# Openings of modulated stages: weight splits pulled forward, none among the normed tiles, gated products spread

## The chip, the cores and the metric

One core of one Trainium2 chip runs the whole program. The metric is device time in microseconds of one execution; the time before is a median of three runs, and one more execution was recorded by the hardware profiler.

## The reference, cut to what matters

The program is two transformer blocks of depth 2 on 256 tokens of width 1024, in fp32. Three of the six sublayer kinds open with the same step, and the change touches only that step:

```
mod = (silu(c) @ ada_w[layer] + ada_b[layer])           # shift, scale, gate for 3 sublayers
h = rms_norm(x, norm_g[layer, i]) * (1 + scale_i) + shift_i
x = x + 0.5 * gate * ((silu(h @ Wa) * (h @ Wb)) @ w_down)   # feed-forward, d_ff = 2816
x = x + gate * diff_attention(h, ...)                       # layer 0
x = x + gate * hgrn2(h, ...)                                # layer 1
```

The six sublayers with a modulation run first, in the order ffn00, attn1, ffn01, ffn10, hgrn, ffn11. The second block (attn2, peer0, conv, peer1) has no modulation, and the change doesn't touch it.

## The kernel before

**Tiling.** Activations lie feature-major: 8 tiles of 128 features x 256 tokens, `xt`. Every product is done in three passes of fp32r: activations and weights are each split into a high part (`xh`, `whi`) and a low part (`xl`, `wlo`), and `mm3` issues high-high, low-high, high-low. A weight *piece* is 128 x 1024 (8 blocks of 128 x 128). Its split is one ACT copy (`whi`) and, after that, one DVE subtraction (`wlo`). A *product* of one piece is 8 x 3 = 24 matmuls. Pieces and products are numbered from 0 in each stage, so that piece 7 is the eighth.

**The order of splits.** All engines execute in the order in which the program writes their instructions. `take` fetches the next piece; before it returns, it writes splits of the coming pieces, as many as `self.ahead` allows beyond the piece taken and as the buffers have room for: six buffers in a feed-forward stage (3 base, 3 of the stage), five in attn1, four in hgrn. The plan of pieces also has *ada* rows in it, from the ninth piece of a stage on: one DVE multiply-and-sum of 128 x 1024 each, for the modulation of a later stage. They are executed in their turn among the splits.

**The opening**, `enter`. The norm's scale (one number per token) isn't known when a stage begins, since it needs the last tile of `xt`. So the first four products are done on tiles that are not normed (`unnormed`: gain only, two extra columns for the shift), and corrected by `complete` after the end. In order: `group` does products 0 and 1 together, k by k; `rstd` (four small matmuls on the sum of squares `ss`, then Ln and Exp on ACT and three small DVE steps, `rsq`); product 2; `rstd_rows` (four matmuls that spread the scale over the partitions, an ACT copy); product 3; `normed_pair`, which makes the 8 normed tiles (DVE `t`, ACT `xh`, DVE `xl` for each) while products 4 and 5 run on them k by k, as they come. In ffn00, the first stage, the squares were summed by PE, and `rstd` has no matmuls of its own.

**After the opening** come the four `complete` (DVE product and a column copy, ACT addition), and in a feed-forward stage `glu(f)`: ACT `sa` (silu, which needs a load of ACT's tables), DVE `t` = sa x pb, ACT `gh`, DVE `gl`. Products 6 and on use four PSUM banks in turn: product 10 writes the bank of product 6, 12 that of 8.

**How far ahead.** `AHEAD = (2, 3, 3, 3)` is the value of `ahead` for the group, product 2, product 3 and the normed pair; afterwards it is 100 (as many as there is room for). Counting `take`'s condition through, the splits stand thus in a feed-forward stage: to piece 3 in front of the group, 4 and 5 in front of product 2, 6 in front of product 3, and 7 and 8 in `normed_pair`, between the first `t` and the first `xh`; 9 to 11 in front of product 6, after `glu` 0, 1 and 2.

Of the kernel before, what the change touches and what calls it, by code (L numbers as in the profile page):

```python
# [83 lines left out]
LAST = 2  # L84
PEER_LAST = 3

AHEAD = (2, 3, 3, 3)


N_FREE, N_SHARED = 11, 48  # L90
# [246 lines left out]
def moving(pool, n, name):  # L337

    t = pool.tile([P, MOVE + n * T], F32R, name=name)
    return t[:, MOVE:].rearrange("p (a b) -> p a b", b=T)  # L340


class Kernel:
# [515 lines left out]
    def enter(self, names, dest):  # L859

        self.ahead = AHEAD[0]
        ps = self.group(names[:2], self.cols, "e")
        y = self.rstd()
        self.ahead = AHEAD[1]
        ps.append(self.features(*names[2], self.cols, "e"))
        self.rstd_rows(y)
        self.ahead = AHEAD[2]
        ps.append(self.features(*names[3], self.cols, "e"))
        self.ahead = AHEAD[3]
        two = self.normed_pair(names[4:6])  # L870
        self.ahead = 100
        return [self.complete(p, d) for p, d in zip(ps, dest)] + two
# [80 lines left out]
    def ffn(self, s):  # L953
        nc, wk = self.nc, self.wk
        layer, sub = SUB[s]
        self.banks(p=range(4), x=range(4, 8), e=range(4), n=[4, 5], ms=[6, 7])
        with self.tc.tile_pool(name=s, bufs=1) as pool:
            gh = moving(pool, KF, "gh")
            gl = moving(pool, KF, "gl")

            def glu(f, pa, pb):
                sa = pool.tile([P, T], F32, name="sa", bufs=2)
                nc.scalar.activation(sa, pa[:, :T], AF.Silu)
                g = wk.tile([P, T], F32, name="t", bufs=3)
                nc.vector.tensor_mul(g, sa, pb[:, :T])
                self.halves(gh[:, f], gl[:, f], g)

            un = [pool.tile([P, T], F32, name="un", bufs=4) for _ in range(4)]
            first = self.enter([(s + "_in", i) for i in range(6)], un)
            for f in range(3):  # L970
                glu(f, first[2 * f], first[2 * f + 1])
            for f in range(3, KF):
                pa = self.features(s + "_in", 2 * f)
                pb = self.features(s + "_in", 2 * f + 1)
                glu(f, pa, pb)
            nc.scalar.preload_act_table_set(LN_EXP)
            gt = self.gate(layer, sub, 0.5)
            if self.next is not None:
                self.lead(self.next)
            py = {}  # L980
            for i, (j, k) in enumerate(DOWN):
                if i % 8 == 0:
                    h, l = self.take(s + "_dn", i // 8)
                if k == 0:
                    py[j] = self.bank("x")
                self.mm3(py[j][:, :T], h[:, i % 8], l[:, i % 8], gh[:, k], gl[:, k], k == 0, k == KF - 1)
                if k == KF - 1:
                    self.resid(j, py[j][:, :T], gt)
# [1070 lines left out]
```

## Time and profile before

| | |
|---|---|
| median of 3 runs | 2886.76 us (2880.81 to 2913.92) |
| the profiled execution, its own time | 2896.64 us |
| its span in the profile | 2894.9 us |
| PE busy | 2833.7 us, 98% of the span |
| DVE, ACT busy | 2175.1 us (75%), 1667.1 us (58%) |

The span runs from the first to the last instruction. PE is TensorE's matmuls, PEld its weight loads, DVE is VectorE, ACT ScalarE. The share of busy time is a mean over all stages; the openings are short stretches of some 25 us each.

### The profile page before, as it was taken

What the parts mean: (1) busy time and instruction counts of PE and PEld (TensorE: products, weight loads), DVE (VectorE), ACT (ScalarE), POOL (GpSimd) and SP (SyncE); (2) the same over time, 40 slices, a digit from 0 to 9 for tenths busy, and PEclk for the clock granted to TensorE, in tenths of its full rate; (3) what the DMA queues carried; (4) which work ended last, traced back from release to release, by engine and by line L of the source; (5) the groups of instructions that cost most, each with busy time, mean ns of one, the idle gap of its engine ahead of it and who ended that gap; (6) DMA issues with size and microseconds to landing.
All of it is one profiled execution on the core that took longest, in us unless ns stands there. A gap on an engine that the chain in (4) does not pass through costs nothing.

```text
span 2894.9 us, 61164 instructions
## 1 busy us (share of the span) xinstructions
PE 2833.7 (98%) x24416; PEld 2787.4 (96%) x24416; DVE 2175.1 (75%) x4491; ACT 1667.1 (58%) x3234; POOL 12.2 (0%) x20
## 2 busy tenths in 40 slices
PE   5999999999999999999999999999999999999999
PEld 5999899999999999799999999999999999999999
DVE  6877788788797656779889755656879889865654
ACT  4456655454566544664688655545464688755553
POOL 0000000000000000000000000000000000000000
PEclk9999999999999999999999999999999999999999
DMA  7985469779543654155544555666445544555664
GB/s 270 332 326 181 145 236 334 281 259 337 193 145 135 201 183 158 53 176 190 185 163 162 173 192 196 213 196 217 156 168 190 190 161 161 170 195 193 214 196 148
DMA packets 158991, 577.17 MB, mean 199 GB/s; under 512 B 17649, under 2 KB 19825, under 8 KB 158321
## 3 DMA queue, kind: packets, MB, share of 16 engines
q1 hardware_dynamic: 156096, 565.25, 58.0%
q0 software_dynamic: 1280, 6.30, 0.6%
q8 instruction: 191, 3.13, 0.4%
q10 hardware_dynamic: 1328, 1.71, 0.2%
q14 instruction: 96, 0.78, 0.1%
HBM read 570.57 MB, written 2.62 MB: 198 GB/s over the span
## 4 chain that ended last, share of the span: by engine, by line
PE 93%; DVE 3%; ACT 2%; issue 1%; DMA 1%; ACTq 0%; DVEq 0%
PE bank L247 93%; DVE wlo L247 1%; DVE xl L247 1%; DMA params<-par 1%; ACT whi L247 1%; DVE t L247 1%; DVE ada_scr L247 1%; ACT un L247 0%; ACT xh L247 0%; ACT L247 0%; DMA raw<-ffn_in 0%; ACT gh L247 0%; ACT hx L247 0%; DVE ss L247 0%; DVE xt L247 0%
## 5 line engine op out<-in xcount | busy, mean ns | idle before, releaser
L247 PE MATMUL bank<-xh,whi 128*128 128x256 f32 (+1 forms) x6272 | 1769.9, 282 | 12.5 <-ACT xh L247 8.7
L247 PE MATMUL bank<-xl,whi 128*128 128x256 f32 (+1 forms) x6272 | 1748.8, 279 | 11.6 <-DVE xl L247 10.9
L247 PE MATMUL bank<-xh,wlo 128*128 128x256 f32 (+1 forms) x6272 | 1746.1, 278 | 2.2 <-DVE wlo L247 2.2
L247 DVE TENSOR_TENSOR wlo<-raw,whi 128x1024 fp32r<-128x1024 f32 x932 | 1134.2, 1225 | 511.2 <-ACT whi L247 503.9
L247 ACT ACTIVATE whi<-raw 128x1024 fp32r<-128x1024 f32 x932 | 972.8, 1056 | 676.4 <-PE bank L247 575.6
L247 PEld LDWEIGHTS bank<-xh,whi 128*128 128x128 f32 x6272 | 1186.4, 189 | 19.1 <-ACT xh L247 10.2
L247 PEld LDWEIGHTS bank<-xl,whi 128*128 128x128 f32 x6272 | 1186.7, 189 | 15.7 <-DVE xl L247 14.3
L247 PEld LDWEIGHTS bank<-xh,wlo 128*128 128x128 f32 x6272 | 1187.3, 189 | 2.8 <-DVE wlo L247 2.8
L247 PE MATMUL bank<-gh,whi 128*128 128x256 f32 x704 | 196.9, 280 | 0.0
L247 PE MATMUL bank<-gl,whi 128*128 128x256 f32 x704 | 196.9, 280 | 0.0
L247 PE MATMUL bank<-gh,wlo 128*128 128x256 f32 x704 | 196.9, 280 | 0.0
L247 DVE SCALAR_TENSOR_TENSOR ada_scr<-raw,cact 128x1024 f32<-128x1024 f32 x144 | 175.6, 1219 | 8.3 <-ACT cact L247 6.1
L247 ACT ACTIVATE ql<-q,gl 128x128 f16<-128x128 f16 x512 | 162.5, 395 | 0.0
L247 ACT ACTIVATE gh<-t 128x256 fp32r<-128x256 f32 x88 | 36.8, 418 | 195.2 <-DVE t L247 195.2
L247 PEld LDWEIGHTS bank<-gh,wlo 128*128 128x128 f32 x704 | 133.7, 190 | 0.0
L247 PEld LDWEIGHTS bank<-gh,whi 128*128 128x128 f32 x704 | 132.9, 189 | 0.0
L247 PEld LDWEIGHTS bank<-gl,whi 128*128 128x128 f32 x704 | 132.1, 188 | 0.0
L247 ACT ACTIVATE slots<-bank 128x256 f32<-128x256 f32 (+38 forms) x296 | 86.4, 294 | 16.2 <-PE bank L247 15.8
L247 PE MATMUL bank<-oh,whi 128*128 128x256 f32 x256 | 73.4, 287 | 0.2 <-ACT hx L247 0.2
L247 PE MATMUL bank<-qh,pm 128*128 128x128 f16 x512 | 72.9, 222 | 0.3
L247 PE MATMUL bank<-ql,pm 128*128 128x128 f16 x512 | 71.5, 219 | 0.1
L247 PE MATMUL bank<-ol,whi 128*128 128x256 f32 x256 | 71.4, 279 | 0.0
(235 smaller groups left out, 2546.8 us busy)
## 6 DMA issues: line engine op xcount, KB each, us to landing
raw<-peer_u SPq DMA_DIRECT2D x256, 512.0 KB, 3.3
raw<-peer_v SPq DMA_DIRECT2D x256, 512.0 KB, 3.7
raw<-ffn_in SPq DMA_DIRECT2D x176, 512.0 KB, 5.1
raw<-ada SPq DMA_DIRECT2D x144, 512.0 KB, 5.3
raw<-ffn_dn SPq DMA_DIRECT2D x88, 512.0 KB, 5.3
raw<-peer_q SPq DMA_DIRECT2D x32, 512.0 KB, 3.4
raw<-conv_in SPq DMA_DIRECT2D x24, 512.0 KB, 4.4
raw<-attn_qk SPq DMA_DIRECT2D x16, 512.0 KB, 4.3
```

The lines of the kernel that those rows point to most:

```text
L247: result = real(*args, **kw)
```

## The change

It does four things. In the stages with a modulation, `ahead` is 4 during the group, so that pieces 4 and 5 are split in front of products 0 and 1 (where the buffers have room). `rstd` is written in the middle of the group, ahead of its fifth k, except in ffn01 and ffn11. `ahead` is 0 in the normed pair, so that no piece is split there: 7 and 8 come after it, in the next `take`, which is product 6's. And `glu(1)` and `glu(2)` no longer stand in front of product 6: `glu(1)` is written after product 6, `glu(2)` after product 8.

```diff
-AHEAD = (2, 3, 3, 3)
+AHEAD = (4, 3, 3, 0)
+
+STAT = 4
...
     def enter(self, names, dest):
 
         self.ahead = AHEAD[0]
-        ps = self.group(names[:2], self.cols, "e")
-        y = self.rstd()
+        found = []
+
+        def statistics(k):
+            if k == STAT and self.stage not in ("ffn01", "ffn11"):
+                found.append(self.rstd())
+
+        ps = self.group(names[:2], self.cols, "e", statistics)
+        y = found[0] if found else self.rstd()
         self.ahead = AHEAD[1]
...
             first = self.enter([(s + "_in", i) for i in range(6)], un)
-            for f in range(3):
-                glu(f, first[2 * f], first[2 * f + 1])
+            glu(0, *first[0:2])
             for f in range(3, KF):
                 pa = self.features(s + "_in", 2 * f)
+                if f < 5:
+                    glu(f - 2, *first[2 * f - 4:2 * f - 2])
                 pb = self.features(s + "_in", 2 * f + 1)
                 glu(f, pa, pb)
```

## Rows read from the trace of the kernel before

**Rows 1.** The page, part 1: busy time, share and instructions of each engine.

```profile
PE 2833.7 (98%) x24416; PEld 2787.4 (96%) x24416; DVE 2175.1 (75%) x4491; ACT 1667.1 (58%) x3234; POOL 12.2 (0%) x20
```

**Rows 2.** The waits of PE: what for, us in total, times, longest.

```profile
PE bank L247 <- DVE xl L247: 10.9, 6, 2.1
PE bank L247 <- ACT xh L247: 8.7, 7, 2.3
```

**Rows 3.** Timeline of PE, ffn10: start, duration, instruction, [idle before <- releaser].

```profile
580.12 0.50 PE L247 MATMUL bank<-ones_d,ss 128*128 128x1 f32 x4
...
587.79 0.39 PE L247 MATMUL bank<-xh,whi 128*128 128x256 f32 x1 [0.81 <-ACT xh L247]
590.21 0.58 PE L247 MATMUL bank<-xl,whi 128*128 128x256 f32 x1 [2.03 <-DVE xl L247]
...
611.73 0.38 PE L247 MATMUL bank<-xh,whi 128*128 128x256 f32 x1 [0.53 <-DVE t L247]
```

**Rows 4.** Windows of ffn10: length, busy (count) by engine, granted clock, DMA.

```profile
590.20:593.10 2.90, 2.89 (x13) 2.89 (x14) 2.90 (x8) 1.76 (x5) 0.00 (x0) 0.51 0.80 280
593.10:597.00 3.90, 3.90 (x37) 3.90 (x36) 3.66 (x13) 2.38 (x6) 0.00 (x0) 1.00 0.14 58
```

**Rows 5.** Timeline of ACT, ffn10.

```profile
575.76 1.04 ACT L247 ACTIVATE whi<-raw 128x1024 fp32r<-128x1024 f32 x1
580.66 0.26 ACT L247 ACTIVATE rsq<-bank,eps 128x2 f32<-128x2 f32 x1 [3.86 <-PE bank L247]
...
584.39 2.94 ACT L247 ACTIVATE whi<-raw 128x1024 fp32r<-128x1024 f32 x3
587.24 0.50 ACT L247 ACTIVATE xh<-t,shift 128x256 fp32r<-128x256 f32 x1
...
597.80 1.28 ACT L247 ACT_TABLE_LOAD   x1
599.09 0.42 ACT L247 ACTIVATE sa<-un 128x256 f32<-128x256 f32 x1
...
613.93 0.36 ACT L247 ACTIVATE sa<-bank 128x256 f32<-128x256 f32 x1
```

**Rows 6.** Timeline of DVE, ffn10.

```profile
585.47 1.23 DVE L247 TENSOR_TENSOR wlo<-raw,whi 128x1024 fp32r<-128x1024 f32 x1 [0.97 <-ACT whi L247]
586.62 0.48 DVE L247 SCALAR_TENSOR_TENSOR t<-xt,gain,ss 128x256 f32<-128x256 f32 x1
587.01 2.36 DVE L247 TENSOR_TENSOR wlo<-raw,whi 128x1024 fp32r<-128x1024 f32 x2
...
589.68 0.48 DVE L247 SCALAR_TENSOR_TENSOR xl<-t,shift,xh 128x256 fp32r<-128x256 f32 x1
...
595.15 0.48 DVE L247 SCALAR_TENSOR_TENSOR xl<-t,shift,xh 128x256 fp32r<-128x256 f32 x1 [0.24 <-ACT xh L247]
...
603.28 1.22 DVE L247 SCALAR_TENSOR_TENSOR ada_scr<-raw,cact 128x1024 f32<-128x1024 f32 x1
...
604.42 1.22 DVE L247 TENSOR_TENSOR wlo<-raw,whi 128x1024 fp32r<-128x1024 f32 x1
...
611.26 0.41 DVE L247 TENSOR_TENSOR t<-sa,bank 128x256 f32<-128x256 f32 x1
612.16 0.42 DVE L247 TENSOR_TENSOR gl<-t,gh 128x256 fp32r<-128x256 f32 x1 [0.48 <-ACT gh L247]
```

**Rows 7.** Timeline of DVE, last step of the scale: ffn00, then ffn01.

```profile
49.34 0.16 DVE L247 SCALAR_TENSOR_TENSOR rsq<-rsq 128x2 f32<-128x2 f32 x1
...
388.67 0.16 DVE L247 SCALAR_TENSOR_TENSOR rsq<-rsq 128x2 f32<-128x2 f32 x1
```

**Rows 8.** Timeline of PE, matmuls that spread the scale: ffn00, then ffn01.

```profile
49.63 0.63 PE L247 MATMUL bank<-ident,rsq 128*128 128x128 f32 x4
...
390.48 0.61 PE L247 MATMUL bank<-ident,rsq 128*128 128x128 f32 x4
```

**Rows 9.** Timeline of DVE, ffn11, after the first three gated products.

```profile
960.07 4.63 DVE L247 TENSOR_TENSOR wlo<-raw,whi 128x1024 fp32r<-128x1024 f32 x4 [0.53 <-ACT whi L247]
```

## The prediction

> **What bounds the kernel now.** I read the page first, then the waits of PE, then the timelines of PE, ACT and DVE over the six openings. The page says that PE is busy for 2833.7 of the 2894.9 us [rows 1]; by its count one matmul takes 2833.7 / 24416 = 0.116 us, so a product takes 2.8 us. PE is therefore the bound, and the change can win only where PE waits: 61 us in all. The waits that it aims at are those for `xl` and `xh`, 19.6 us in total [rows 2]; the rest is mostly the start of ffn00, before any product runs. In ffn10 the reader sees two of them, 0.81 us for the first normed `xh` and 2.03 us for the first `xl` [rows 3]. The cause stands in the other two timelines: DVE does two splits (7 and 8) between the first `t` and the second, 2.27 us, and ACT three (6 to 8) ahead of the first normed `xh` [rows 5, 6]. After that stop the granted clock is 0.51 for 2.9 us and then 1.00 [rows 4], that is the lower of the two levels, 1.2 GHz, and then 2.4. So a stop there costs twice: 13 matmuls take 2.9 us where they take 13 x 0.116 = 1.5, so another 1.4 us.
>
> **The change, part by part, in ffn10.**
>
> *Pieces 4 and 5 forward.* Two splits move into a hole: ACT is idle for 3.86 us before the `rsq` at 580.66 [rows 5]. With them ACT works from 575.76 to 578.7 (three splits at 0.97, the pitch of the three at 584.39), DVE to about 580.3 (three at 1.14, the step from 603.28 to 604.42 [rows 6]). Price nothing; cover gone, the two would cost DVE's 2.3 us. In attn1 there is room for piece 4 only, and in hgrn for neither, so there the part does nothing. No SP or POOL step moves with it but the loads that follow each split into its freed buffer, two earlier by some 5 us.
>
> *The statistic in the middle of the group.* Four small matmuls move up by 24 matmuls; PE's work is the same. PE now waits there for `ss`: the square ends about when ACT's split starts, 575.8, the sum 0.6 us later at 576.4, and the middle of the group is 580.12 - 24 x 0.116 = 577.3 [rows 3, 5]. Cover 0.9 us; without it PE stops, and everything behind it in the group. The gain is nothing either, since the scale was not late in this stage: the next wait of PE is for the normed tile [rows 3]. What it does is to keep the two pulled splits from delaying the scale, by about 2 us.
>
> *No split among the normed tiles.* Piece 6 still stands in front of the first `t`, so that stays at 586.62. The first `xh` then runs at 587.07, not 587.24; the second `t` at 587.02; the first `xl` at 587.6, not 589.68: 2.1 us earlier. The last `xl` moves from 595.15 to 593.1. PE's stop shrinks from 0.81 and 2.03 us to about 0.7 and 0.4. I take the clock as kept, since no stop is left that is as long as 2.03 us. The normed pair would end 0.57 us after the last `xl` (five matmuls), at about 594.2, where it ended at 597.0 [rows 4]: **2.8 us won at this point**.
>
> *Where the two splits go.* They now stand in front of product 6, with 9 to 11, and behind `complete` and `glu(0)`: on ACT behind four additions, the table load (597.80, 1.28 us), `sa` at 599.09, the wait for DVE's `t`, and `gh` [rows 5]. Product 7 runs at once after product 6, so it needs piece 7 at 597.0. Take the last `xl` as zero (595.15 before, 593.1 after). `sa` comes at 3.94 [rows 5, 6], `gh` ends at 5.2, so `whi` 7 is there at 6.2, that is 599.3, and `wlo` 7 at 7.4, 600.5. PE waits 2.3 us, runs two matmuls, and waits 0.95 us. Product 7 ends at 603.1, against 597.0 + 2 x 2.8 = 602.6 before: the 2.8 us are gone, and 0.5 besides. If the clock falls as it did after the old stop, it is 1.4 more, 1.9. Before, product 7 had its piece from the normed pair; this is what the two splits paid for.
>
> *A rule that speaks against this place.* The table load is 1.28 us in the trace, and the next activation starts 0.01 us behind it [rows 5]. The Trainium skill, "ScalarE: Activation LUTs", What ACT_TABLE_LOAD costs, counts a drain of 1.38 us besides and 2.66 us for a switch. By that, piece 7 would come 1.4 us later in each of the six openings, all of which load a table, and the time would be 8 us higher, 2905. By that rule the trace disagrees: the row leaves it no chance, and the sum goes by the row.
>
> *The gated products spread.* `glu(1)` no longer delays product 6's splits, which saves product 7 some 1.25 us, and `glu(2)` the same; that is in the numbers above. But a bank comes free only when its `glu` has read it. DVE from 6.25 on: five splits and two ada rows (7 x 1.14), to 14.25; `t` and `gl` of `glu(1)`, 0.9 and 0.35 (611.26, 612.16 [rows 6]); an ada and split 12, to 17.75; `t` of `glu(3)`, at 610.9, about where it was (611.26); `gl`, to 19.0; an ada and split 13, to 21.3; and only then `glu(2)`, behind whose `gh` (22.1) stand split 14 on ACT (to 23.0) and `sa` of `glu(4)`. That `sa` reads product 8's bank, which product 12 writes. It ran at 613.93 [rows 5]; now it ends at 23.4, 616.5. Product 12 started one product after 611.73 [rows 3], at 614.5. **ffn10: 2.0 us lost**, and this wait swallows whatever the clock cost before it. In other words, a feed-forward stage loses 4.1 us by the new place of the splits and of `glu(2)`, and wins what the first `xl` gains.
>
> *The loads.* Two raw buffers come free some 13 us later, so two loads do; they are for pieces eight further on, and the DMA share behind the opening is 0.14 [rows 4]. Nothing; without that cover, a later split would wait.
>
> **The other openings.** In ffn01 the statistic stays behind the group, and the two pulled splits stand in front of its Ln and its DVE steps: the scale is ready 2 x 1.14 us later than 388.83, at 391.1, and PE wants it at 390.48 [rows 7, 8]. So 0.7 of the 2.1 us are lost there: 4.1 - 1.4 = 2.7 lost. ffn00 is in the middle of the group on paper only: its statistic needs no matmul, and Ln and Exp stand behind the two splits on ACT (2 x 0.97), while PE wanted the scale as soon as it was there (49.34 + 0.16 against 49.63). PE waits 1.9 us, DVE makes up 0.4, so the first `xl` gains 0.6; one ada fewer stands in the way (0.7 in the end, since products become the bound): 4.1 - 0.7 - 0.6 = 2.8 lost. In ffn11 no ada stands among the splits [rows 9], so the banks don't bind, and product 7 does: by ffn10's 0.5 to 1.9 us and 0.7 for the scale as in ffn01, 1.2 to 2.6; 2.0. In attn1 and hgrn the normed tiles lose one or two splits (about 2 us won), and piece 7 waits behind the table load there as well, but no `glu`; the nearest rows are ffn10's, from which I bound each between 0.5 won and 1.9 lost, and take 0.3 lost, near the end at which the clock holds.
>
> **The sum.** 2.8 + 2.7 + 2.0 + 2.0 + 0.6 = 10.1 us slower, 0.35%. Against the profiled execution that is 2896.6 + 10 = 2907. The median of the runs is 9.9 us lower than that execution, so the predicted median is 2886.8 + 10 = 2897. The three runs lie within 33 us, so about 1% is what can be told from no change.
>
> **The rivals.**
>
> *The stops vanish and nothing takes their place.* Product 7's piece is in time, because ACT and DVE reach it sooner than by my chain, or because products run later. Then the six openings win 2.8 in ffn10, about 2 each in attn1 and hgrn, and in ffn01, ffn11 and ffn00 2.8 less the scale's delay (2.1, 2.1, 0.9): 12 us, 2875. For it: DVE is idle in parts of that stretch. Against it: the order of the program, by which no split of piece 7 can precede `gh` of `glu(0)`.
>
> *The banks don't bind.* If DVE runs 2 to 3 us ahead of my chain (an ada less, a shorter hop), only product 7's stop stays: 0.5 in ffn10, 1.2 in ffn01, 1.5 in ffn00 and ffn11, and nothing in the other two. 5 us slower, 2892. This is also the case in which the change hardly does what it says: stops only move.
>
> *DVE becomes the bound of the feed-forward stages.* Behind the opening a pair of products is 5.6 us of PE and, on DVE, two splits, 1.33 ada rows and a `glu` (3.33 x 1.14 + 1.25), 5.05 us. It catches up 0.5 us a pair only. If `glu(4)` to `glu(6)` come late too, each of the three feed-forward stages with ada rows stops twice more for some 1.5 us, and attn1, hgrn and ffn11 pay the clock: 10 + 9 + 3 = 22 us slower, 2909. It decides from the point where an `sa` is late by more than 0.5 us.
>
> **How the numbers follow.** Forecast 0.45, the first rival 0.15, the second 0.25, the third 0.15. The forecast alone reaches from 2885 to 2909, with 12 us either way for the median of so few runs. For 8 in 10 it goes to the first rival's time below, 2875, less 1, and above to the third's with a little of the scatter, 2913. Faster by over 1% needs a time under 2858, which no case gives; slower by over 1% one above 2916, at the far end of the third: 0.02 and 0.06.
>
> **What would show it.** In the new trace: in the normed pairs no wait of PE over 1 us, and the first `xl` 1 to 2 us sooner after the group; in each opening PE waiting some 2 us for ACT `whi` and 1 us for DVE `wlo` in product 7, with a lower clock behind it; in ffn10 and ffn01 a wait for ACT `sa` at product 12; in ffn00 and ffn01 a wait of PE for `rsq`. The prediction is wrong if product 7 starts without a wait, or if PE's busy stretch after the opening is not broken before product 13.

## The result and the profile after

The changed kernel takes 2906.43 us (median of 19 runs, 2896.08 to 2921.25) against 2886.76 us for 19 runs of the kernel before (2871.48 to 2915.46). The ratio is 1.0068, with a 95% interval of 1.0049 to 1.0086: 19.7 us slower, where 10.1 were forecast. The time lies in the forecast's range, on its slow side.

The page after, part 1, answers [rows 1]; the waits of PE under it answer [rows 2] (what for, us in total, times, longest). In all listings of the changed kernel the helper's line is L249, where it was L247 (L250 in the composites at the end).

```profile
PE 2834.0 (98%) x24416; PEld 2784.0 (96%) x24416; DVE 2174.6 (75%) x4491; ACT 1666.3 (57%) x3234; POOL 12.3 (0%) x20
```

```profile
PE bank L249 <- ACT whi L249: 10.7, 6, 2.2
...
PE bank L249 <- DVE wlo L249: 5.3, 8, 0.8
PE bank L249 <- ACT hx L249: 3.7, 2, 3.5
PE bank L249 <- DVE rsq L249: 3.0, 3, 1.4
PE bank L249 <- ACT sa L249: 2.8, 4, 1.3
```

PE's work is the same, 24416 matmuls, so the loss is in its waits and in the clock behind them (in a single execution also in the distance at which matmuls follow each other, of which more below). The 10.9 us for `xl` are gone from the list. In their place stand 10.7 us for `whi`, six times, once an opening, new waits for `rsq` and `sa`, and a long one for `hx` (3.5 us; before, three, the longest 0.7). All but the one for `hx` are in the forecast. Their places in ffn10 show on PE's timeline (start, duration, instruction, [idle before <- releaser]), which answers [rows 3]:

```profile
593.44 0.38 PE L249 MATMUL bank<-xh,whi 128*128 128x256 f32 x1 [0.78 <-ACT xh L249]
...
605.16 0.39 PE L249 MATMUL bank<-xh,whi 128*128 128x256 f32 x1 [2.15 <-ACT whi L249]
...
606.42 0.38 PE L249 MATMUL bank<-xh,wlo 128*128 128x256 f32 x1 [0.76 <-DVE wlo L249]
...
615.26 0.39 PE L249 MATMUL bank<-xh,whi 128*128 128x256 f32 x1 [0.62 <-ACT sa L249]
...
622.30 0.38 PE L249 MATMUL bank<-xh,whi 128*128 128x256 f32 x1 [1.32 <-ACT sa L249]
```

The normed pair has one stop of 0.78 us; the 2.03 us for the first `xl` is gone. Product 7 stops at 605.16 for `whi` 7 and, two matmuls on, for `wlo` 7. Products 10 and 12 stop for the `sa` that reads the bank they write. The timelines of ACT and DVE behind it answer [rows 5, 6]; first ACT, then DVE:

```profile
601.54 1.28 ACT L249 ACT_TABLE_LOAD   x1
602.84 0.42 ACT L249 ACTIVATE sa<-un 128x256 f32<-128x256 f32 x1
...
604.07 4.84 ACT L249 ACTIVATE whi<-raw 128x1024 fp32r<-128x1024 f32 x5
...
621.88 0.36 ACT L249 ACTIVATE sa<-bank 128x256 f32<-128x256 f32 x1
```

```profile
598.90 0.48 DVE L249 SCALAR_TENSOR_TENSOR xl<-t,shift,xh 128x256 fp32r<-128x256 f32 x1 [0.24 <-ACT xh L249]
...
605.14 2.36 DVE L249 TENSOR_TENSOR wlo<-raw,whi 128x1024 fp32r<-128x1024 f32 x2 [0.52 <-ACT whi L249]
```

Count from the last `xl`, 598.90, as the prediction did. The splits start 5.2 us behind it (5.2 forecast for the end of `gh`), the first is done at some 605.1, 6.2 (6.2), and `sa` of `glu(4)` ends at 621.88 + 0.36 = 622.24, 23.3 behind it (23.4).

What was not forecast stands in attn1. Its timelines, PE first, then ACT:

```profile
262.16 0.39 PE L249 MATMUL bank<-xh,whi 128*128 128x256 f32 x1 [0.70 <-ACT whi L249]
...
263.42 0.58 PE L249 MATMUL bank<-xh,wlo 128*128 128x256 f32 x1 [0.76 <-DVE wlo L249]
...
271.28 0.58 PE L249 MATMUL bank<-xh,whi 128*128 128x256 f32 x1 [3.52 <-ACT hx L249]
```

```profile
261.03 3.92 ACT L249 ACTIVATE whi<-raw 128x1024 fp32r<-128x1024 f32 x4
...
269.01 1.06 ACT L249 ACTIVATE whi<-raw 128x1024 fp32r<-128x1024 f32 x1 [3.67 <-DMA raw<-attn_qk]
...
270.76 0.47 ACT L249 ACTIVATE hx<-bank,qg 128x256 f32<-128x256 f32 x1
```

PE waits 3.52 us for an `hx` that frees a bank. ACT ran it late because it stands behind a split on that engine, and the split waited 3.67 us for its raw load. The load was late because SP, which issues the loads in order, waited for a raw buffer. First SP's waits in 226 to 290 us of the kernel before, then of the changed one, and under them SP's timeline there after:

```profile
SPq L247 <- DVE wlo L247: 24.7, 14, 4.2
```

```profile
SPq L249 <- DVE wlo L249: 46.3, 14, 13.6
```

```profile
245.25 4.43 SPq L249 DMA_DIRECT2D raw<-attn_qk  x2
263.39 0.33 SPq L249 DMA_DIRECT2D raw<-ada  x1
264.53 1.47 SPq L249 DMA_DIRECT2D raw<-attn_qk  x2
```

Between 249.7 and 263.39 SP issues no load. Behind the stop the clock is low, as windows of attn1 show (length; busy and count of PE, PEld, DVE, ACT, POOL; granted clock; DMA share, GB/s); first before, then after:

```profile
270.00:280.00 10.00, 10.00 (x74) 8.61 (x73) 6.55 (x24) 6.94 (x24) 0.00 (x0) 0.95 0.53 173
280.00:290.00 10.00, 10.00 (x60) 9.35 (x61) 7.42 (x27) 5.13 (x13) 0.00 (x0) 0.71 0.27 83
```

```profile
260.00:270.00 10.00, 6.11 (x33) 5.48 (x32) 7.33 (x11) 6.30 (x12) 0.00 (x0) 0.83 0.50 161
270.00:280.00 10.00, 8.72 (x41) 8.72 (x42) 5.00 (x11) 5.16 (x15) 0.00 (x0) 0.51 0.70 261
280.00:290.00 10.00, 10.00 (x66) 8.92 (x65) 4.38 (x16) 4.24 (x10) 0.00 (x0) 0.81 0.30 105
290.00:300.00 10.00, 10.00 (x69) 9.59 (x70) 9.02 (x44) 9.93 (x35) 0.00 (x0) 0.83 0.01 2
```

A table of the six openings shows how much longer each stretch became, read from the starts of the matmuls on PE's timeline, from the first group to the normed pair, from there to product 6, to 14, and to 20 (488 matmuls in both kernels, 448 in ffn00). In ffn10 the four stretches took 13.47, 9.19, 23.33 and 16.96 us before and 13.42, 6.69, 27.93 and 16.96 after. In some stretches the steady distance of two matmuls is 118 ns in one execution and 113 in the other (the last section says more of this). From product 6 to 20, 217 matmuls of ffn01 and 336 of ffn11 stand at the longer distance before, and 3 and 24 after; in hgrn it is 92 before and 198 after. At 4.5 ns each, the loss in the table is 1.0 and 1.4 us above the sum of the stretches in ffn01 and ffn11, and 0.5 below it in hgrn (each figure is rounded by itself).

| opening | to the pair | pair | 6 to 14 | 14 to 20 | loss | forecast |
|---|---|---|---|---|---|---|
| ffn00 | 1.5 | -2.8 | 4.3 | 0.0 | 3.0 | 2.8 |
| attn1 | -0.6 | -1.3 | 9.9 | 0.8 | 8.8 | 0.3 |
| ffn01 | 0.2 | -2.9 | 4.8 | -0.6 | 2.4 | 2.7 |
| ffn10 | 0.0 | -2.5 | 4.6 | 0.0 | 2.0 | 2.0 |
| hgrn | -0.6 | -2.1 | 3.3 | -2.0 | -1.9 | 0.3 |
| ffn11 | 1.3 | -3.1 | 2.6 | -0.6 | 1.5 | 2.0 |
| sum | | | | | 15.8 | 10.1 |

In the openings, what is missing in the forecast is attn1. Its 8.8 us do not all stay: from product 20 to the next stage it takes 74.50 us for 77.15, so that the stage as a whole loses 6.1 (151.85 us for 145.73). Thus the trace gives the change some 13 us.

The rest of the 19.7 is not shown to be the change's. The two profiled spans differ by 9.2 us (2904.1 and 2894.9); 6423 matmuls before and 4066 after stand at the longer distance, 10.6 us at 4.5 ns, so that at equal distances they would differ by 19.8. Of this some 6 us are a lower clock behind ffn11's opening, where PE's waits are the same in both executions: it costs 5.7 us there before and 12.0 after, and between 0 and 12 in the 14 kernels profiled. How much of such clock the median of many runs has is not known; the interval of the ratio is 14 to 25 us.

### The profile page after: what moved, and what is told of

It reads as the page before. It is cut to its first block, busy times and chain, and to the rows that moved or that the text cites. A ratio compares the mean times of both kernels' runs of the same rounds, so it can differ in the third digit from the quotient of the medians.

```text
span 2904.1 us, 61169 instructions
## 1 busy us (share of the span) xinstructions
PE 2834.0 (98%) x24416; PEld 2784.0 (96%) x24416; DVE 2174.6 (75%) x4491; ACT 1666.3 (57%) x3234; POOL 12.3 (0%) x20
## 4 chain that ended last, share of the span: by engine, by line
PE 91%; DVE 4%; ACT 3%; issue 1%; DMA 1%; ACTq 0%; DVEq 0%
PE bank L249 91%; DVE wlo L249 1%; ACT whi L249 1%; DVE xl L249 1%; DVE t L249 1%; DMA params<-par 1%; DVE ada_scr L249 1%; ACT xh L249 0%; ACT L249 0%; ACT un L249 0%; DMA raw<-attn_qk 0%; DMA raw<-ffn_in 0%; DVE ss L249 0%; DVE xt L249 0%; DVE m L249 0%
## 5 line engine op out<-in xcount | busy, mean ns | idle before, releaser
L249 PE MATMUL bank<-xh,whi 128*128 128x256 f32 (+1 forms) x6272 | 1767.5, 282 | 25.6 <-ACT whi L249 10.7
L249 PE MATMUL bank<-xl,whi 128*128 128x256 f32 (+1 forms) x6272 | 1748.0, 279 | 1.6
L249 PE MATMUL bank<-xh,wlo 128*128 128x256 f32 (+1 forms) x6272 | 1744.0, 278 | 5.3 <-DVE wlo L249 5.3
L249 DVE TENSOR_TENSOR wlo<-raw,whi 128x1024 fp32r<-128x1024 f32 x932 | 1133.7, 1225 | 523.0 <-ACT whi L249 515.1
L249 ACT ACTIVATE whi<-raw 128x1024 fp32r<-128x1024 f32 x932 | 971.5, 1056 | 667.3 <-PE bank L249 568.4
L249 PEld LDWEIGHTS bank<-xh,whi 128*128 128x128 f32 x6272 | 1186.0, 189 | 33.9 <-ACT whi L249 11.8
L249 PEld LDWEIGHTS bank<-xl,whi 128*128 128x128 f32 x6272 | 1186.1, 189 | 6.3 <-DVE xl L249 4.3
L249 PEld LDWEIGHTS bank<-xh,wlo 128*128 128x128 f32 x6272 | 1184.5, 189 | 6.9 <-DVE wlo L249 6.9
L249 PE MATMUL bank<-gh,whi 128*128 128x256 f32 x704 | 195.2, 277 | 0.0
L249 PE MATMUL bank<-gl,whi 128*128 128x256 f32 x704 | 195.2, 277 | 0.0
L249 PE MATMUL bank<-gh,wlo 128*128 128x256 f32 x704 | 195.2, 277 | 0.0
L249 DVE SCALAR_TENSOR_TENSOR ada_scr<-raw,cact 128x1024 f32<-128x1024 f32 x144 | 175.5, 1219 | 8.4 <-ACT cact L249 6.2
L249 ACT ACTIVATE ql<-q,gl 128x128 f16<-128x128 f16 x512 | 162.6, 396 | 0.0
L249 ACT ACTIVATE gh<-t 128x256 fp32r<-128x256 f32 x88 | 36.8, 418 | 197.8 <-DVE t L249 197.8
L249 PEld LDWEIGHTS bank<-gh,whi 128*128 128x128 f32 x704 | 132.9, 189 | 0.0
L249 PEld LDWEIGHTS bank<-gl,whi 128*128 128x128 f32 x704 | 132.1, 188 | 0.0
L249 PEld LDWEIGHTS bank<-gh,wlo 128*128 128x128 f32 x704 | 132.1, 188 | 0.0
L249 ACT ACTIVATE slots<-bank 128x256 f32<-128x256 f32 (+38 forms) x296 | 86.8, 296 | 16.7 <-PE bank L249 16.5
L249 PE MATMUL bank<-oh,whi 128*128 128x256 f32 x256 | 74.4, 291 | 0.2 <-ACT hx L249 0.2
L249 PE MATMUL bank<-qh,pm 128*128 128x128 f16 x512 | 72.9, 222 | 0.3
L249 PE MATMUL bank<-ol,whi 128*128 128x256 f32 x256 | 71.9, 281 | 0.0
L249 PE MATMUL bank<-oh,wlo 128*128 128x256 f32 x256 | 71.9, 281 | 0.0
```

Of the source, the lines that this page charges most:

```text
L249: result = real(*args, **kw)
```

## The experiments

The theory: in the feed-forward stages the new place of pieces 7 and 8 and the late gated products cost some 2 to 3 us each, about as forecast; in attn1 the same new place keeps raw buffers busy, a load comes late, and that costs some 9 us in its opening. The rivals are named with each run. All ratios are to the kernel before; 0.001 is 2.9 us.

**attn1 as before.** The opening of attn1 alone gets its old splits and its old statistic (the lines left out put `ahead` for `AHEAD` at the other three places).

```diff
-        self.ahead = AHEAD[0]
+        ahead = AHEAD if self.stage != "attn1" else (2, 3, 3, 3)
+        self.ahead = ahead[0]
...
-            if k == STAT and self.stage not in ("ffn01", "ffn11"):
+            if k == STAT and self.stage not in ("ffn01", "ffn11", "attn1"):
...
```

> The changed kernel, with attn1's opening as it was before the change (splits 2, 3, 3, 3 ahead, the statistic behind the group). My theory: attn1 alone gave some 9 of the 19.7 us, since with no split between its group and product 6 its raw buffers come free some 11 us late, a load lands late, and the bank of product 8 with it. Then the PE wait of 3.5 us for `hx` is gone, and the run comes to about 11 us above the kernel before, ratio 1.004 (1.002 to 1.005). Rival, that attn1's stop belongs to one execution only, or that the loss sits in the feed-forward stages: the run stays at 1.006 to 1.008.

Measured: 1.005 (1.0024 to 1.0075), 5 us below the changed kernel. PE's longest wait for `hx` is 0.7 us, and the opening takes 67.09 us for 77.36 (the whole stage 143.6 for 151.9). In the trace the theory holds; the times alone do not settle it, since the two intervals overlap.

**Two more raw buffers in attn1.** Nothing else is changed, and the splits stay late.

```diff
-MORE = {"ffn00": (5, 3, 3), "ffn01": (5, 3, 3), "ffn10": (5, 3, 3), "ffn11": (5, 3, 3), "attn1": (2, 2, 2),
+MORE = {"ffn00": (5, 3, 3), "ffn01": (5, 3, 3), "ffn10": (5, 3, 3), "ffn11": (5, 3, 3), "attn1": (4, 2, 2),
```

> The changed kernel, with two more raw buffers in attn1 (7 for 5), nothing else. If the late load is what stops product 8 there, its load is issued in time, PE's wait of 3.5 us for `hx` goes, and with it the half clock behind it: some 7 us less, ratio 1.004 (1.003 to 1.005). If the cause is the four splits that stand in a row on ACT in front of product 6, and not the load, buffers change nothing: the wait for `hx` stays above 2 us and the ratio at 1.006 to 1.008. In both the wait of 0.7 us for `whi` 7 stays.

Measured: 1.0035 (1.0012 to 1.0058), 9.5 us below the changed kernel. ACT's timeline in attn1 and the window behind it:

```profile
261.01 3.92 ACT L249 ACTIVATE whi<-raw 128x1024 fp32r<-128x1024 f32 x4
...
265.23 1.05 ACT L249 ACTIVATE whi<-raw 128x1024 fp32r<-128x1024 f32 x1
```

```profile
270.00:280.00 10.00, 10.00 (x83) 9.09 (x83) 8.56 (x27) 5.46 (x15) 0.00 (x0) 1.00 0.96 363
```

The same four splits in a row, but the fifth starts at 265.23 without a wait, 3.8 us sooner. PE waits 0.71 us for `hx`, the clock is 1.00, the opening takes 65.38 us and the stage 142.5. In the trace the load was the cause of this stop, not the row of splits on ACT; by the times alone it is not settled here either, since the intervals overlap.

**The kernel before with these buffers.**

```diff
-MORE = {"ffn00": (5, 3, 3), "ffn01": (5, 3, 3), "ffn10": (5, 3, 3), "ffn11": (5, 3, 3), "attn1": (2, 2, 2),
+MORE = {"ffn00": (5, 3, 3), "ffn01": (5, 3, 3), "ffn10": (5, 3, 3), "ffn11": (5, 3, 3), "attn1": (4, 2, 2),
```

> The kernel before, with two more raw buffers in attn1 (7 for 5). In the changed kernel the two buffers took 12 us out of attn1's opening. If they repair only what the change broke, the kernel before gains nothing, ratio 0.999 to 1.001 and attn1's opening near 68.6 us; if attn1 was short of raw buffers before as well, its opening falls to about 65.5 us and the ratio to 0.998 to 0.999.

Measured: 1.0009 (0.9974 to 1.0045), attn1's opening 66.93 us. In one execution it is 1.7 us shorter than before, against 12.0 us in the changed kernel; the time shows no gain. Even the 1.7 us are within what one opening differs by between executions (one and the same code of attn1's opening took 65.42 us in the run below with the splits among the normed tiles and 68.77 in the first composite). The shortage is mostly one that the change made.

**Two places, two orders.** Three runs and the changed kernel make a square: the splits of pieces 7 and 8 among the normed tiles or behind them, the gated products 1 and 2 in front of product 6 or spread. All four have the pulled splits and the moved statistic.

The gated products go back in front:

```diff
-            glu(0, *first[0:2])
+            for f in range(3):
+                glu(f, first[2 * f], first[2 * f + 1])
...
-                if f < 5:
-                    glu(f - 2, *first[2 * f - 4:2 * f - 2])
```

The splits go back among the normed tiles:

```diff
-AHEAD = (4, 3, 3, 0)
+AHEAD = (4, 3, 3, 3)
```

The first edit alone:

> The changed kernel, with the gated products of pairs 0 to 2 all in front of product 6 again, as before the change. My chain: `whi` of pieces 6 and 7 then stands behind two more gated products on ACT and DVE, so that PE's wait in product 7 grows from 2.2 + 0.8 to some 4.5 to 5.5 us; the waits for `sa` at products 10 and 12 (0.6 and 1.3 us in ffn10) go. Net 0 to 1.5 us a stage more: ratio 1.007 to 1.009. Rival, that the banks are what costs and the spread is the mistake: the wait in product 7 grows by less than 1 us, and the ratio falls to 1.004.

The second alone:

> The changed kernel with the splits among the normed tiles put back (4, 3, 3, 3 ahead); the pulled splits 4 and 5, the statistic in the middle of the group and the spread gated products stay. My theory has the loss in the place of pieces 7 and 8: product 7's waits for `whi` and `wlo` go in all six openings and attn1's wait for `hx` too; the stops among the normed tiles (0.8 and 2.0 us in ffn10) come back; what stays is the later scale in ffn00, ffn01 and ffn11, some 3 us together. Ratio 1.000 to 1.002. Rival, that the pulled splits and the moved statistic cost: above 1.003.

Both:

> The kernel before, with only the pulled splits 4 and 5 and the statistic in the middle of the group (4, 3, 3, 3 ahead; the gated products all in front of product 6 as before). The run that kept the old place of the splits but spread the gated products came out at 1.0037 and showed six waits for `sa`, 5.4 us, and three for `rsq`, 2.8 us. If those are what was left, this one keeps the `rsq` waits and loses the `sa` waits: 3 us above the kernel before, ratio 1.000 to 1.002. Rival, that the spread of the gated products is a gain whatever stands before it, as it was with the moved splits (where putting them back cost 14 us more): ratio 1.005 or more, by a wait in products 7 to 9.

| | gated products in front | spread |
|---|---|---|
| splits among the normed tiles | 1.0007 (0.998 to 1.0033) | 1.0037 (0.9998 to 1.0076) |
| splits behind them | 1.0117 (1.0079 to 1.0155) | 1.0068 (1.0049 to 1.0086) |

With the splits behind the pair and the gated products in front, product 7 of ffn10 stops so:

```profile
617.58 0.58 PE L249 MATMUL bank<-xh,whi 128*128 128x256 f32 x1 [4.52 <-ACT whi L249]
...
618.84 0.58 PE L249 MATMUL bank<-xh,wlo 128*128 128x256 f32 x1 [0.47 <-DVE wlo L249]
```

That is 5.0 us for 2.9, inside what was expected; the time went past its upper end. Going back costs 14 us by the mean values, so the rival (the spread is the mistake) falls. The second run came out above what was expected, with its mean in the rival's range, that the pulled splits and the moved statistic cost; the third, which has both and came out at 1.0007, speaks against that rival. With the splits in their old place it is the other way round by the mean values, 1.0037 spread and 1.0007 in front, though these intervals overlap. The waits of PE say why: the first list is of the run with the spread, the second of the one without.

```profile
PE bank L249 <- ACT sa L249: 5.4, 6, 1.3
PE bank L249 <- DVE rsq L249: 2.8, 3, 1.3
```

```profile
PE bank L249 <- DVE rsq L249: 3.0, 3, 1.5
```

The second has no wait for `sa`. What the pulled splits and the moved statistic cost by themselves is the wait for `rsq`, 3 us, and by the time nothing that can be told from zero. The spread is worth 2 us a stage where product 7 waits for a split behind it, and costs what the `sa` waits cost where it doesn't.

**The normed tiles alone.** The kernel before with one number changed.

```diff
-AHEAD = (2, 3, 3, 3)
+AHEAD = (2, 3, 3, 0)
```

> The kernel before with one number changed: no split among the normed tiles (2, 3, 3, 0 ahead). No statistic is moved, no split pulled, no gated product spread. Only pieces up to 5 or 6 are split before the pair, so product 6 or 7 finds none of its pieces, behind three gated products. My chain: a wait of about 5 us in product 6 or 7 of each feed-forward stage, against 2 to 3 us won, attn1 as bad as in the changed kernel: 20 to 30 us above the kernel before, ratio 1.007 to 1.011. Rival, that the moved statistic and the pulled splits are what costs in the changed kernel: ratio below 1.004.

Measured: 1.0062 (1.0037 to 1.0087), a little under what was expected and above the rival's 1.004, though the interval touches it. PE's waits for `whi`:

```profile
PE bank L247 <- ACT whi L247: 20.7, 6, 4.6
```

Product 7 waits 4.63 us in each feed-forward stage, and attn1's opening takes 76.71 us. So this one number alone costs as much as the whole change, and the other parts bring little or give a part back.

**The gated products later.** The banks that products 10 and 12 need are those of `glu(3)` and `glu(4)`; `glu(1)` and `glu(2)` hold none of them.

```diff
-                if f < 5:
-                    glu(f - 2, *first[2 * f - 4:2 * f - 2])
+                if f in (6, 9):
+                    glu(f // 3 - 1, *first[2 * (f // 3) - 2:2 * (f // 3)])
```

> The changed kernel, with the gated products of pairs 1 and 2 in pairs 6 and 9 in place of 3 and 4. If the `sa` waits come from these two standing ahead of pairs 3 and 4, whose banks products 10 and 12 need, they go (0.6 and 1.3 us in ffn10, 0.7 in ffn01), and the stop in product 7 stays at 2.2 and 0.8 us: ratio 1.005 to 1.0065. Rival, that the late splits themselves put DVE behind: the `sa` waits stay, or the time moves to `wlo`, and the ratio is 1.0065 to 1.008.

Measured: 1.0062 (1.0031 to 1.0093). The time can't be told from that of the changed kernel; the waits can:

```profile
PE bank L249 <- ACT sa L249: 0.8, 2, 0.4
```

`sa` falls from 2.8 to 0.8 us, `whi` stays (10.8 us). The cause of the bank waits is shown: the two gated products ahead of pairs 3 and 4.

**Pieces 6 and 7 earlier.** They are split in front of product 2, so that nothing is left for product 7. Two runs, with the gated products spread and in front.

```diff
-AHEAD = (4, 3, 3, 0)
+AHEAD = (4, 5, 4, 0)
```

> The changed kernel with 4, 5, 4, 0 ahead: pieces 6 and 7 are split in front of product 2, ahead of the statistic's last steps, so that neither the first `t` nor product 7 waits for a split; only piece 8 is left for behind the pair (in attn1 the raw buffers let piece 7 come in front of product 3). My theory, that the place of these two splits is the whole loss: no wait above 1 us in the normed pair nor in product 7, 3 us less per feed-forward opening than the kernel before, attn1 as before; the `sa` waits stay at 1 to 2 us a stage: ratio 0.997 to 1.000. Rival, that DVE has no room for two more splits there and the scale comes 2.3 us later in all stages: `rsq` waits of 2 us and a ratio above 1.003.

> The same with the gated products of pairs 0 to 2 all in front of product 6 again. If the spread costs a wait for `sa` wherever product 7 has its piece already, this run is 4 to 6 us faster than the one with the spread, ratio 0.995 to 0.998. Rival: `whi` of piece 8 stands behind three gated products and product 8 stops for it, so the run is slower than the one with the spread by as much.

Measured: 1.0028 (1.0003 to 1.0053) and 1.0042 (1.0016 to 1.0067). Both expectations were missed. The waits of PE, first with the spread, then without:

```profile
PE bank L249 <- ACT sa L249: 8.8, 6, 2.2
PE bank L249 <- ACT hx L249: 4.8, 2, 4.6
```

```profile
PE bank L249 <- ACT whi L249: 8.3, 5, 1.9
PE bank L249 <- ACT hx L249: 5.0, 2, 4.8
```

The feed-forward part came in part: ffn10's opening takes 60.98 and 60.96 us for 62.95 before (some 0.5 of it by the steady distance of matmuls), with no stop over 0.5 us in its pair or product 7. What ate it is above all attn1, which I had put at "as before": it still has no split among its normed tiles, its loads are still late (in the first of the two runs SP issues none from 248.2 to 261.9 us), and its opening takes 75.28 and 74.90 us. `rsq` costs 3.0 us more. And both orders have their price: 8.8 us for `sa`, or 8.3 for `whi` of piece 8.

**A composite.** Each opening gets what the runs above left without a stop.

```diff
-AHEAD = (4, 3, 3, 0)
+AHEAD = {"ffn00": (2, 5, 4, 0), "ffn01": (2, 5, 4, 0), "ffn11": (2, 5, 4, 0), "ffn10": (4, 5, 4, 0),
+         "attn1": (4, 3, 3, 3), "hgrn": (4, 3, 3, 0)}
...
-            if k == STAT and self.stage not in ("ffn01", "ffn11"):
+            if k == STAT and self.stage not in ("ffn00", "ffn01", "ffn11"):
...
-                if f < 5:
-                    glu(f - 2, *first[2 * f - 4:2 * f - 2])
+                if f in (6, 9):
+                    glu(f // 3 - 1, *first[2 * (f // 3) - 2:2 * (f // 3)])
```

> For each opening what the runs so far left without a stop: in the feed-forward stages pieces 6 and 7 are split in front of product 2 (ffn00, ffn01 and ffn11 take 4 and 5 there as well, behind the statistic's own steps), attn1 splits 4, 3, 3, 3 ahead with the statistic in the middle, hgrn as in the changed kernel; and the gated products of pairs 1 and 2, whose data lie outside the four banks that products 6 on take in turn, come as late as pairs 6 and 9. By my theory no `sa` wait above 0.5 us, no `rsq` wait, no stop in product 7 or 8 of a feed-forward stage, attn1 some 3 us shorter than in the kernel before: 10 to 14 us below it, ratio 0.995 to 0.997. Rival, that DVE's backlog is only put off and stops PE later in the stage: ratio 1.000 or more, with waits for `wlo` or `sa` behind product 10.

Measured: 0.9977 (0.9944 to 1.0009); some half of what was expected, and not to be told from the kernel before. attn1's opening, expected 3 us shorter, takes 68.77 us for 68.58. Its waits for `sa`:

```profile
PE bank L250 <- ACT sa L250: 4.7, 6, 1.6
```

The longest, in ffn00, follows the gated product put into pair 6. A last run puts the two into pairs 9 and 12, and gives attn1 the two raw buffers.

```diff
-                if f in (6, 9):
-                    glu(f // 3 - 1, *first[2 * (f // 3) - 2:2 * (f // 3)])
+                if f in (9, 12):
+                    glu(f // 3 - 2, *first[2 * (f // 3) - 4:2 * (f // 3) - 2])
...
-MORE = {"ffn00": (5, 3, 3), "ffn01": (5, 3, 3), "ffn10": (5, 3, 3), "ffn11": (5, 3, 3), "attn1": (2, 2, 2),
+MORE = {"ffn00": (5, 3, 3), "ffn01": (5, 3, 3), "ffn10": (5, 3, 3), "ffn11": (5, 3, 3), "attn1": (4, 2, 2),
```

> The composite, with the gated products of pairs 1 and 2 put off to pairs 9 and 12 and two more raw buffers in attn1. In the composite six `sa` waits, 4.7 us, were left, the longest 1.6 us behind the one put into pair 6: there DVE had not caught up yet. If it has by pair 9, these waits shrink to 1 to 2 us and the run comes out 10 to 14 us below the kernel before, ratio 0.995 to 0.997. If DVE has no slack in these stages at all, the waits move to pairs 9 to 12 with the same length, and the ratio stays at 0.9975 or above.

Measured: 0.9951 (0.9921 to 0.998), 14 us faster than the kernel before. The `sa` waits are halved:

```profile
PE bank L250 <- ACT sa L250: 2.3, 5, 0.7
```

ffn10's opening takes 57.25 us, 5.7 less than before (some 0.5 of them by the steady distance of matmuls in that execution). attn1's takes 68.90, so the two buffers brought nothing there. So the aim of the change was sound; its order of work was not.

## Why the prediction was right, and where it was wrong

*The direction and the mechanism in the feed-forward stages* were right. The split of 7 and 8 left the normed tiles, the 2.03 us stop went, and product 7 stopped for `whi` and `wlo`: 2.15 + 0.76 us for 2.3 + 0.95 forecast. The chain on ACT and DVE ran to 0.1 us as worked out. Restoring the splits took the product 7 stops away, moving them alone made them. In attn1 and hgrn the wait for `whi` was shorter, 0.70 and 1.49 us.

*The rsq waits* came in ffn00, ffn01 and ffn11, 1.44, 0.53 and 1.04 us (1.9, 0.7, 0.7 forecast):

```profile
51.52 0.60 PE L249 MATMUL bank<-ident,rsq 128*128 128x128 f32 x3 [1.44 <-DVE rsq L249]
...
399.78 0.49 PE L249 MATMUL bank<-ident,rsq 128*128 128x128 f32 x2 [0.53 <-DVE rsq L249]
...
947.73 0.49 PE L249 MATMUL bank<-ident,rsq 128*128 128x128 f32 x2 [1.04 <-DVE rsq L249]
```

*The bank wait* at product 12 came, in ffn10, 1.32 us, and one at product 10 as well. The forecast had both gated products late there; the runs with later gated products show them as the cause. The stage lost 2.0 us as forecast, and all four feed-forward stages 8.9 us for 9.5.

*The clock behind product 7* did not fall in ffn10: 1.00 from 602 to 612 us. The forecast had put that fall in a condition, and the bank wait covered it, so the sum is the same. In ffn00 and ffn01 it did fall, which cost some 1.7 us in ffn01 (2.9 x 0.30 + 3.3 x 0.26, from the granted clock of 415.8 to 418.7 and to 422.0 us), and the waits for `sa` were 0.15 and 0.72 us only. That these two stages came near their forecast, 3.0 and 2.4 us for 2.8 and 2.7, is thus in part luck: there the clock cost what the forecast had put on the bank. The table load took 1.28 us and the activation behind it started 0.02 us later, as the row of before had it. By the rule of the Trainium skill ("ScalarE: Activation LUTs", What ACT_TABLE_LOAD costs), a drain of 1.38 us would have stood between; the trace disagrees again.

*The step that failed* is the one on the loads: "Two raw buffers come free some 13 us later, so two loads do ... Nothing". In ffn10 it holds; there are eight raw buffers. It was not asked again for attn1, which has five: there the cover that the sentence asks for is missing, the fifth split waits for its load, and `hx` behind it on ACT holds product 8's bank. attn1 was put at 0.3 us lost, between 0.5 won and 1.9 lost, by ffn10's rows. Its opening lost 8.8: 3.5 in the stop for `hx`, and most of the rest in the clock. By an estimate from the windows (busy time times the part of the clock that is missing) the half clock cost before, in 270 to 290 us, 10 x (0.05 + 0.29) = 3.4 us, and after, in 260 to 300, 6.1 x 0.17 + 8.7 x 0.49 + 10 x (0.19 + 0.17) = 8.9, so 5.5 more. The two waits in product 7, 1.5 us, are paid by the 1.9 us won ahead of product 6. The bound of 1.9 us was wrong since it came from a stage whose loads are never late. Two more buffers gave back 9.5 us by the ratios, and 9.4 us of the stage in the trace.

*hgrn* won 1.9 us, past the 0.5 that the bounds allowed. Up to product 14 it lost 0.6 (-0.6, -2.1 and 3.3), as bounded; the rest comes behind it, where a wait for `wlo` in product 15 that took 1.68 us before takes 0.34. The prediction did not follow this stage so far.

*The rivals.* That nothing takes the place of the stops is refuted by six waits in product 7. That the banks don't bind is refuted by `sa` in ffn10 and ffn01. That DVE becomes the bound of the feed-forward stages had the nearest time, 2909, by another road than the true one: the four waits for `sa` stand at products 10 and 12 and none behind them, so DVE did catch up. Its 2909 sets the upper end of the stated range; the forecast with its own scatter ends at 2909, close above the measured 2906.4, so part of the margin is owed to a road that was not taken.

What stays open: how much of attn1's clock is owed to the stop, and how much would have been lost in this stage anyway; and what the 6 us or so are that the medians show beyond the trace's 13. The kernel before, with no such stop, also has 0.71 in 280 to 290 us.

## What to carry to other kernels

A split moved behind a stretch of work also moves the freeing of its buffer, and with it the load that waits for the buffer; ask how many buffers each stage has, not only the one that was read. A step moved out of one stop must have a place that is earlier than its own user: here piece 7 shortened ffn10's opening when it went ahead of the pair, and lengthened the run when it went behind it. Work that holds no scarce buffer (here the gated products of pairs 1 and 2) can go last; work that holds a bank (pairs 3 and 4) goes first.

## What the runs showed of the hardware

Matmuls of the same kernel, back to back and at a granted clock of 1.00, come at two distances. Windows of 100 us in the same code, first in the kernel before, then in the changed one:

```profile
1000.00:1100.00 100.00, 100.00 (x851) 100.00 (x850) 57.31 (x71) 47.57 (x67) 0.00 (x0) 1.00 0.59 184
```

```profile
1000.00:1100.00 100.00, 100.00 (x885) 100.00 (x884) 60.36 (x77) 50.66 (x71) 0.00 (x0) 1.00 0.62 194
```

100 us over 851 is 117.5 ns, over 885 113.0 ns. In the profiled executions of 14 kernels this window holds 851, 852, 884 or 885 matmuls and nothing between; one of them had 113 ns in 500 to 560 us and 117.5 here, four the reverse. A distance can hold for 200 us and more, changes within an execution (also inside the openings above), and differs between executions. It is 4% of such a stretch, enough for the spread of 1% between runs of one kernel, and it is why single spans mislead here: the kernel with pieces 6 and 7 earlier and the gated products in front (ratio 1.0042) had a profiled span of 2882.5 us, 12 below that of the kernel before. What sets it is not shown.

The granted clock does not follow the length of a stop alone. Before, PE was busy 0.39 of the 2.5 us ahead of 590.2, and the clock behind was 0.51 [rows 4]. After, product 7 stops for the same two waits in ffn01 and in ffn10, 2.15 and 0.76 us, with nearly the same busy time of PE ahead of and between them. In ffn01 (the first two rows) the clock fell, to 0.70 in the mean of the second row and 0.74 in the 3.3 us behind it; in ffn10 (the last two) it stayed:

```profile
412.70:415.80 3.10, 1.03 (x10) 0.84 (x8) 0.85 (x2) 2.60 (x5) 0.00 (x0) 1.00 0.01 3
415.80:418.70 2.90, 2.05 (x9) 1.85 (x10) 2.83 (x3) 2.90 (x5) 0.00 (x0) 0.70 0.22 56
```

```profile
602.00:605.10 3.10, 1.01 (x9) 0.81 (x8) 0.85 (x2) 2.60 (x5) 0.00 (x0) 1.00 0.00 0
605.10:608.00 2.90, 2.08 (x15) 1.88 (x16) 2.86 (x3) 2.90 (x5) 0.00 (x0) 1.00 0.22 58
```

Of the six stops in product 7 of the changed kernel, those in ffn00, attn1 and ffn01 were followed by the lower clock and those in ffn10, hgrn and ffn11 were not. What decides it is not shown.
